# Two plain gate tiles instead of four in each SwiGLU, and q and k of the stick-breaking heads stacked by DMA

## The chip, the core and the metric

The kernel runs on one core of a Trainium2 chip. The metric is the device time of one execution in microseconds (us), the median of several runs. The engines of the core are TensorE (PE, the matmuls), VectorE (DVE), ScalarE (ACT), GpSimd (POOL) and SyncE (SP), which issues nearly all transfers. They run side by side and wait for each other by semaphores; each works through its own list of instructions in order.

## What is computed

A decoder trunk of two layers on 512 tokens of width 1024, float32. Each layer is SwiGLU, a mixer, SwiGLU; the first mixer is a hybrid of a recurrent block and attention, the second is stick-breaking attention with 16 heads of width 64.

```
def _swiglu(h, w_in, w_out):
    a, b = jnp.split(h @ w_in, 2, axis=-1)
    return (jax.nn.silu(a) * b) @ w_out
...
        z = jnp.einsum('bhqd,bhkd->bhqk', qi, k).astype(jnp.float32) * scale
        log_nb = jnp.where(mask, jax.nn.log_sigmoid(-z), 0.0)
        after = lax.cumsum(log_nb, axis=3, reverse=True) - log_nb
        w = jnp.where(mask, jnp.exp(jax.nn.log_sigmoid(z) + after), 0.0)
        return jnp.einsum('bhqk,bhkd->bhqd', w.astype(v.dtype), v)
...
    for layer in range(DEPTH):
        x = x + 0.5 * _swiglu(_rmsnorm(x, ffn_norm[layer, 0]), ffn_w_in[layer, 0], ffn_w_out[layer, 0])
        ...
        x = x + 0.5 * _swiglu(_rmsnorm(x, ffn_norm[layer, 1]), ffn_w_in[layer, 1], ffn_w_out[layer, 1])
```

The inner width of a SwiGLU is 2816, so 22 tiles of 128 (below: gate tiles, or gates 0 to 21).

## The kernel before

Activations lie transposed, features on the 128 partitions and the 512 tokens in the free dimension, in eight tiles `x`. To keep float32 accuracy with the fast matmul format every operand is split in two, a rounded high part (ScalarE's cast) and the rest (VectorE's subtraction), and each product is three matmuls (high by high, high by low, low by high). So every weight tile of 128x1024 costs a load of 512 KB, a cast and a subtraction.

**A SwiGLU** (`ffn(f, ...)`, f = 0 to 3) works on the gate tiles in two ways.

- *Plain* (`plain(j, rb)`, for j below `PLAIN`): 24 matmuls of 512 columns for the half a and 24 for the half b, on the unnormed activations `xh`, `xl`. The norm's factor of each token, `rb`, comes out during gate 0: TensorE sums squares (`rstd_parts`), GpSimd takes the root, TensorE spreads it, ScalarE copies it. `normed` multiplies the results by `rb` afterwards, and `gate` applies silu, the product of the halves, and the split of the hidden tile.
- *In pairs* (`pair(j, between, operands, before)`): two gate tiles at once (half a and half b as one block row of two) by a seven-product scheme of the Strassen kind on blocks. Each of the seven calls of `product(pt, w, o, start)` is 24 matmuls of 256 columns. Its weights are blocks a11, a12, a21, a22 or sums of them (s1 to s4: VectorE's `add`), split by `parts`. Its activations are seven operands, t0 to t6 (`ops`), blocks or sums of blocks of the normed activations, made once per SwiGLU by the generator `g_inputs(rb)`: `quarter` (four pieces of 256 columns), `less` (a difference), `put` (the split). The pair pulls one step of it ahead of each product (`next(operands, 0)`). The order of the products is: operand 0, 1, 4, 5, 2, 6 and, as `tail`, 3. The tail is run behind the first product of the next pair.

The output product (`outputs(c, done)`) of a chunk of four gates is eight tiles of 12 matmuls of 512 columns. Chunk c-1's outputs are spread between the products of the pairs of chunk c (`between(i)`, by the table `OUTPUTS`); `CHUNKS` says which gates belong to a chunk. With `PLAIN = 4` chunk 0 is plain and chunks 1 to 4 are pairs.

**Stick-breaking attention** (`stick`) goes through 8 pairs of heads. `qk_tile(p)` projects q and k of a pair (24 matmuls each); its `evac` takes the result out of the accumulator: it makes the tiles `qks` of head e and head o, each a stack of two halves of 64 partitions (for q the high part on one half and the low part on the other; for k the high part on both), and for k the low parts `klo` (named `kl0e` to `kl1o` in the trace), whose other half is zero. The score is then two matmuls, `qks` by `qks` and `qks` by `klo`. Before, the stacks are made by ScalarE copies and VectorE subtractions of 64 partitions each. `attend` runs 64 score blocks in a row; `Fill` pulls projections of later pairs and output products in between, by the due times `need`. The hybrid layer's attention makes its stacks with `stack`, four transfers issued by SyncE.

What sets the order: TensorE's order is the order of the program text (`manual_schedule`). The lists of the other engines and of SyncE are ordered by the framework's scheduler by its own estimate of times, and are fixed when the program is built. Buffers that matter here: `raw` 3 (loaded weights), `hi` and `lo` 4 each (split weights), `sum` 4, `mm` 3 and `s` 2 accumulators.

Of the kernel before, what the change touches and what calls it, by code (L numbers as in the profile page):

```python
# [10 lines left out]
F32 = mybir.dt.float32  # L11
F32R = mybir.dt.float32r
AF = mybir.ActivationFunctionType
ALU = mybir.AluOpType
AX = mybir.AxisListType

P = 128
S = 512
# [5 lines left out]
HD = 64  # L24
# [17 lines left out]

PLAIN = 4
CHUNKS = [(0, 4), (4, 8), (8, 12), (12, 16), (16, 22)]

OUTPUTS = [((0, 1, 2, 1, 1), (1, 0, 1, 0, 1)), ((0, 0, 2, 0, 2), (1, 0, 1, 0, 2)), ((0, 0, 2, 0, 2), (1, 0, 1, 0, 2)),
# [20 lines left out]
def kernel(ctx: ExitStack, tc: tile.TileContext, x, par, ffn_in, ffn_in2, ffn_out, ffn_out2,  # L69
                      hy_ug, hy_qkv, hy_qf, rg_w, hy_out, sb_qk, sb_v, sb_out, out):  # L70
    nc = tc.nc
    V, A, G, T, SY = nc.vector, nc.scalar, nc.gpsimd, nc.tensor, nc.sync
# [219 lines left out]
    def stack(st, h, l):  # L292

        top, low = slice(0, HD), slice(HD, P)
        SY.dma_start(out=st[0][top].bitcast(F32), in_=h[top].bitcast(F32))
        SY.dma_start(out=st[0][low].bitcast(F32), in_=l[top].bitcast(F32))
        SY.dma_start(out=st[1][low].bitcast(F32), in_=h[low].bitcast(F32))
        SY.dma_start(out=st[1][top].bitcast(F32), in_=l[low].bitcast(F32))
# [31 lines left out]
    def ffn(f, g_next, last=False):  # L330
# [3 lines left out]
        with ExitStack() as es:  # L334
# [233 lines left out]
            def tail():  # L568
                pass

            for c in range(1, len(CHUNKS)):
                if f == 0 and c == 3:
                    channel_consts(gp.tile([P, S], F32, tag="p5", bufs=1, name="t4"))
                g = outputs(c - 1, False)
                for j, counts in zip(range(*CHUNKS[c], 2), OUTPUTS[c - 1]):
                    def between(i):
                        for _ in range(counts[i]):
                            next(g)

                    tail = pair(j, between, operands, tail)  # L580
                if c == len(CHUNKS) - 1:
                    tail()
                run(g)
# [482 lines left out]
    def stick(g_next):  # L1066
        with ExitStack() as es:
# [9 lines left out]
            qk, vv = {}, {}  # L1077
# [5 lines left out]
            def qk_tile(p):  # L1083
                def evac(j):
                    def go(pt):
                        nonlocal rt, rb
                        if rb is None:
                            rt, rb = rstd()
                            for c, sg in enumerate((1.0, -1.0)):
                                V.tensor_scalar(out=rs[:, c], in0=rt, scalar1=sg * HD ** -0.5, scalar2=None,  # L1090
                                                op0=ALU.mult)
                        halves = [slice(0, HD), slice(HD, P)]
                        st = [mp.tile([P, S], F32R, tag=f"qk{j}{c}", bufs=2, name="qks") for c in "eo"]
                        if j == 0:

                            for t, a, b in zip(st, halves, halves[::-1]):
                                A.copy(out=t[a], in_=pt[a])
                                V.tensor_tensor(out=t[b], in0=pt[a], in1=t[a].bitcast(F32), op=ALU.subtract)
                            qk[p, j] = st
                        else:  # L1100

                            kt = wk("kt", 1)
                            V.tensor_tensor(out=kt, in0=pt, in1=rb, op=ALU.mult)
                            for t, l, a, b in zip(st, klo[p % 2], halves, halves[::-1]):
                                A.copy(out=t[a], in_=kt[a])
                                V.tensor_tensor(out=l[a], in0=kt[a], in1=t[a].bitcast(F32), op=ALU.subtract)
                                A.copy(out=t[b], in_=kt[a])
                            qk[p, j] = st
                    return go

                return [(1, 24 * US_512, g_proj(sb_qk[p, j], evac(j), on_x, KT)) for j in range(2)]
# [141 lines left out]
```

## Time and profile before

| | |
|---|---|
| median of 3 runs | 1869.08 us (1867.19 to 1870.18) |
| the profiled execution | 1865.11 us, span of its instructions 1863.4 us |
| TensorE matmul busy | 1836.0 us, 99% of the span |
| VectorE busy | 1413.3 us, 76% |
| ScalarE busy | 955.3 us, 51% |
| granted TensorE clock, mean | 1.000 |
| the chain of work that ended last | TensorE 88%, VectorE 6%, ScalarE 2% |

Times inside the trace are us from the start of the span. The four SwiGLUs lie at about 5 to 350, 575 to 930, 920 to 1270 and 1515 to 1860 us; the hybrid mixer between the first two, the stick-breaking attention from about 1270 to 1515. A timeline row gives start, duration, engine, line of the kernel, operation, output and inputs, and in brackets the idle time before it with what ended it. Instructions of one engine overlap a little in such rows, since the next starts while the last one drains; the spacing of the starts is what one costs on a busy engine.

### The profile page before, as it was taken

Reading aid. Unit: us, or ns where it says so; the run is one execution under the profiler, and the core shown is the slowest. Engines: PE = TensorE matmul, PEld = TensorE weight load, DVE = VectorE, ACT = ScalarE, POOL = GpSimd, SP = SyncE. Lnnn points to the kernel's source line nnn. Section 1 sums busy time; section 2 is a strip of 40 time slices with the busy share of each in tenths; the row PEclk is TensorE's granted clock in tenths of the full one; section 3 lists DMA queues with packets and bytes.
Section 4 is the critical chain, followed back from the end, with each engine's and each line's share of the span. In section 5 each row is a group of like instructions: output and inputs, shape, how many; then the busy total and the mean of one; then the engine's idle time right before and its main releaser. Section 6 shows DMA issues by size and latency. Waiting matters only on the chain.

```text
span 1863.4 us, 29383 instructions
## 1 busy us (share of the span) xinstructions
PE 1836.0 (99%) x11818; PEld 1664.1 (89%) x11818; DVE 1413.3 (76%) x1892; ACT 955.3 (51%) x1399; POOL 122.2 (7%) x266
## 2 busy tenths in 40 slices
PE   8999999998999999999999999999999999999999
PEld 6899999898888899999889999988888888999997
DVE  8867776688878877676597777765889978777773
ACT  5444444467755444444454444445777654444441
POOL 2000000111100000000000000001333400000000
PEclk9999999999999999999999999999999999999999
DMA  5332332353233333332323333232212123333322
GB/s 184 102 103 92 104 113 75 95 163 108 81 94 102 102 97 97 102 114 77 128 80 109 106 103 102 88 99 98 69 57 69 57 91 102 97 111 105 96 76 95
DMA packets 57304, 183.65 MB, mean 99 GB/s; under 512 B 8016, under 2 KB 9296, under 8 KB 57168
## 3 DMA queue, kind: packets, MB, share of 16 engines
q1 hardware_dynamic: 57168, 181.77, 30.6%
q8 instruction: 93, 1.52, 0.3%
q14 instruction: 43, 0.35, 0.1%
HBM read 172.31 MB, written 2.10 MB: 94 GB/s over the span
## 4 chain that ended last, share of the span: by engine, by line
PE 88%; DVE 6%; ACT 2%; issue 2%; POOL 1%; DMA 0%; SPq 0%; POOLq 0%; DVEq 0%; ACTq 0%
PE mm L457 22%; PE s L457 11%; PE mm L130 6%; PE mm L132 6%; PE mm L131 6%; PE t L457 5%; PE po L130 4%; PE po L132 4%; PE po L131 4%; PE mm L246 2%; PE mm L248 2%; PE mm L247 2%; PE mm L227 1%; PE mm L228 1%; PE mm L229 1%
## 5 line engine op out<-in xcount | busy, mean ns | idle before, releaser
L446 ACT CAST hi_w<-sum 128x1024 fp32r<-128x1024 f32 x144 | 150.8, 1050 | 191.9 <-PE s L457 52.1
L447 DVE TENSOR_TENSOR lo_w<-sum,hi_w 128x1024 fp32r<-128x1024 f32 x144 | 176.0, 1224 | 95.3 <-ACT hi_w L446 94.7
L122 ACT CAST hi_wo<-raw_wo 128x1024 fp32r<-128x1024 f32 (+1 forms) x96 | 94.1, 980 | 152.4 <-PE mm L131 64.2
L446 ACT CAST hi_w<-raw 128x1024 fp32r<-128x1024 f32 x72 | 75.8, 1052 | 129.9 <-PE s L457 70.7
L123 DVE TENSOR_TENSOR lo_wo<-raw_wo,hi_wo 128x1024 fp32r<-128x1024 f32 (+1 forms) x96 | 108.8, 1133 | 23.7 <-ACT hi_wo L122 23.7
L132 PE MATMUL po<-g,lo_wo 128*128 128x512 f32 x320 | 125.1, 391 | 1.3 <-DVE lo_wo L123 1.3
L130 PE MATMUL mm<-g,hi_wo 128*128 128x512 f32 (+1 forms) x324 | 125.8, 388 | 0.0
L130 PE MATMUL po<-g,hi_wo 128*128 128x512 f32 x320 | 125.6, 392 | 0.0
L132 PE MATMUL mm<-g,lo_wo 128*128 128x512 f32 (+1 forms) x324 | 125.5, 387 | 0.0
L131 PE MATMUL mm<-g,hi_wo 128*128 128x512 f32 (+1 forms) x324 | 125.5, 387 | 0.0
L131 PE MATMUL po<-g,hi_wo 128*128 128x512 f32 x320 | 125.2, 391 | 0.0
L122 ACT CAST hi_w<-raw_w 128x1024 fp32r<-128x1024 f32 (+2 forms) x75 | 77.9, 1040 | 85.3 <-PE mm L131 42.5
L123 DVE TENSOR_TENSOR lo_w<-raw_w,hi_w 128x1024 fp32r<-128x1024 f32 (+2 forms) x75 | 90.7, 1209 | 30.0 <-ACT hi_w L122 29.8
L549 DVE SCALAR_TENSOR_TENSOR x<-mm,x 128x512 f32<-128x512 f32 (+1 forms) x81 | 55.3, 683 | 49.8 <-PE mm L132 49.3
L246 PE MATMUL mm<-hi_w,xh 128*128 128x256 f32 (+1 forms) x312 | 90.8, 291 | 2.2 <-DVE q L897 2.2
L463 DVE TENSOR_TENSOR sum<-a,a 128x1024 f32<-128x1024 f32 x36 | 44.1, 1225 | 58.4 <-DMA a<-in_dram 58.4
L248 PE MATMUL mm<-hi_w,xl 128*128 128x256 f32 (+1 forms) x312 | 88.4, 283 | 0.0
L247 PE MATMUL mm<-lo_w,xh 128*128 128x256 f32 (+1 forms) x312 | 88.2, 283 | 0.0
L447 DVE TENSOR_TENSOR lo_w<-raw,hi_w 128x1024 fp32r<-128x1024 f32 x72 | 87.8, 1219 | 0.0
L549 DVE SCALAR_TENSOR_TENSOR x<-po,x 128x512 f32<-128x512 f32 x80 | 55.1, 689 | 39.5 <-PE po L132 39.5
L457 PE MATMUL s<-t4l,hi_w 128*128 128x256 f32 x288 | 81.6, 283 | 0.0
L457 PE MATMUL s<-t2l,hi_w 128*128 128x256 f32 x288 | 81.4, 283 | 0.0
(480 smaller groups left out, 6314.7 us busy)
## 6 DMA issues: line engine op xcount, KB each, us to landing
raw_w<-in_dram SPq DMA_DIRECT2D x72, 512.0 KB, 3.4
a<-in_dram SPq DMA_DIRECT2D x72, 512.0 KB, 3.5
raw<-in_dram SPq DMA_DIRECT2D x72, 512.0 KB, 3.5
raw_wo<-in_dram SPq DMA_DIRECT2D x64, 512.0 KB, 3.5
raw_wo<-in_dram SPq DMA_DIRECT2D x32, 384.0 KB, 3.0
raw_who<-in_dram SPq DMA_DIRECT2D x16, 512.0 KB, 3.3
qks<-hs SPq DMA_DIRECT2D x24, 128.0 KB, 2.5
x<-in_dram SPq DMA_DIRECT2D x8, 256.0 KB, 4.6
```

Of the source, the lines that this page charges most:

```text
L122: A.copy(out=hi[:, :n], in_=raw[:, :n])
L123: V.tensor_tensor(out=lo[:, :n], in0=raw[:, :n], in1=hi[:, :n].bitcast(F32), op=ALU.subtract)
L130: T.matmul(out=pt, lhsT=ah, rhs=bh, start=(start and i == 0), stop=False)
L131: T.matmul(out=pt, lhsT=ah, rhs=bl, start=False, stop=False)
L132: T.matmul(out=pt, lhsT=al, rhs=bh, start=False, stop=(stop and i == n - 1))
L246: T.matmul(out=pt, lhsT=ah, rhs=bh, start=(k == 0), stop=False)
L247: T.matmul(out=pt, lhsT=ah, rhs=bl, start=False, stop=False)
L248: T.matmul(out=pt, lhsT=al, rhs=bh, start=False, stop=(k == KT - 1))
L446: A.copy(out=hi, in_=src)
L447: V.tensor_tensor(out=lo, in0=src, in1=hi.bitcast(F32), op=ALU.subtract)
L457: T.matmul(out=po, lhsT=a, rhs=b[:, k], start=start and c + k + q == 0, stop=k == 3 and q == 2, skip_group_check=not (start and c == 0))
L549: V.scalar_tensor_tensor(out=xT[d][:, t], in0=po[:, t], scalar=0.5, in1=xT[d][:, t], op0=ALU.mult, op1=ALU.add)
```

## The change

`PLAIN` becomes 2. Gates 0 and 1 of each SwiGLU stay plain; gates 2 and 3 become a pair, run directly behind the plain tiles and without outputs in between, since chunk 0 has no chunk ahead of it. In the attention `evac` splits the whole tile of 128 partitions into `h` and `l` (named `hs` in the trace), one ScalarE copy and one VectorE subtraction, and transfers put the halves in place: four by `stack` for q; four by `stack` and two for `klo` for k.

```
-PLAIN = 4
+PLAIN = 2
...
             def tail():
                 pass
 
+            for j in range(PLAIN, CHUNKS[0][1], 2):
+                tail = pair(j, lambda i: None, operands, tail)
             for c in range(1, len(CHUNKS)):
...
-                        halves = [slice(0, HD), slice(HD, P)]
                         st = [mp.tile([P, S], F32R, tag=f"qk{j}{c}", bufs=2, name="qks") for c in "eo"]
+                        h, l = (mp.tile([P, S], F32R, tag=f"qk{c}", bufs=2, name="hs") for c in "hl")
+                        qk[p, j] = st
                         if j == 0:
 
-                            for t, a, b in zip(st, halves, halves[::-1]):
-                                A.copy(out=t[a], in_=pt[a])
-                                V.tensor_tensor(out=t[b], in0=pt[a], in1=t[a].bitcast(F32), op=ALU.subtract)
-                            qk[p, j] = st
+                            A.copy(out=h, in_=pt)
+                            V.tensor_tensor(out=l, in0=pt, in1=h.bitcast(F32), op=ALU.subtract)
+                            stack(st, h, l)
                         else:
 
                             kt = wk("kt", 1)
                             V.tensor_tensor(out=kt, in0=pt, in1=rb, op=ALU.mult)
-                            for t, l, a, b in zip(st, klo[p % 2], halves, halves[::-1]):
-                                A.copy(out=t[a], in_=kt[a])
-                                V.tensor_tensor(out=l[a], in0=kt[a], in1=t[a].bitcast(F32), op=ALU.subtract)
-                                A.copy(out=t[b], in_=kt[a])
-                            qk[p, j] = st
+                            A.copy(out=h, in_=kt)
+                            V.tensor_tensor(out=l, in0=kt, in1=h.bitcast(F32), op=ALU.subtract)
+                            stack(st, h, h)
+                            for t, a in zip(klo[p % 2], (slice(0, HD), slice(HD, P))):
+                                SY.dma_start(out=t[a].bitcast(F32), in_=l[a].bitcast(F32))
```

On TensorE, at the end of plain gate 1 of the second SwiGLU (`s` is the accumulator of its half b, `xh`, `xl` the activations, t0 operand 0). Before:

```order
L130 MATMUL s<-xh_6010,hi_w 128x512
L131 MATMUL s<-xl_6011,hi_w 128x512
L132 MATMUL s<-xh_6010,lo_w 128x512
L130 MATMUL mm<-xh_5968,hi_w 128x512
L131 MATMUL mm<-xl_5969,hi_w 128x512
L132 MATMUL mm<-xh_5968,lo_w 128x512
```

The same place after the change:

```order
L130 MATMUL s<-xh_6105,hi_w 128x512
L131 MATMUL s<-xl_6106,hi_w 128x512
L132 MATMUL s<-xh_6105,lo_w 128x512
L457 MATMUL mm<-t0h,hi_w 128x256
L457 MATMUL mm<-t0l,hi_w 128x256
L457 MATMUL mm<-t0h,lo_w 128x256
```

Where gate 2 began with the activations, the first product now begins with operand 0.

On VectorE, the list of the second SwiGLU from the split of operand 0 on (`t0l` to `t4l` are low parts of operands; `lo_w` of line 123 is a plain weight's, of line 447 a product's; `ab` and `g` are the plain tiles' norm and gate; `sum` a sum of weight blocks or of activations). Before:

```order
L408 TENSOR_TENSOR t0l<-sum,t0h 128x1024
L408 TENSOR_TENSOR t1l<-sum,t1h 128x1024
L389 TENSOR_TENSOR ab<-mm,rb 128x512
L411 TENSOR_TENSOR t3l<-t3h,sum 128x1024
L123 TENSOR_TENSOR lo_w<-raw_w,hi_w 128x1024
L351 TENSOR_TENSOR ab<-ab 128x512
L408 TENSOR_TENSOR t2l<-t6l,t2h 128x1024
L390 TENSOR_TENSOR ab<-s,rb 128x512
L463 TENSOR_TENSOR sum<-raw,a_6411 128x1024
L123 TENSOR_TENSOR lo_w<-raw_w,hi_w 128x1024
L411 TENSOR_TENSOR t3h<-t6l,t3h 128x1024
L408 TENSOR_TENSOR t4l<-t3l,t4h 128x1024
```

After:

```order
L408 TENSOR_TENSOR t0l<-sum,t0h 128x1024
L463 TENSOR_TENSOR sum<-raw,a_6364 128x1024
L408 TENSOR_TENSOR t1l<-sum,t1h 128x1024
L389 TENSOR_TENSOR ab<-mm,rb 128x512
L411 TENSOR_TENSOR t3l<-t3h,sum 128x1024
L447 TENSOR_TENSOR lo_w<-sum,hi_w 128x1024
L351 TENSOR_TENSOR ab<-ab 128x512
L408 TENSOR_TENSOR t2l<-t6l,t2h 128x1024
L390 TENSOR_TENSOR ab<-s,rb 128x512
L411 TENSOR_TENSOR t3h<-t6l,t3h 128x1024
L408 TENSOR_TENSOR t4l<-t3l,t4h 128x1024
L463 TENSOR_TENSOR sum<-sum,raw 128x1024
```

The operands keep their order and their place in the list nearly unchanged; the two plain splits are gone and a split of a product's weights stands there.

On SyncE, the transfers of the attention (`raw_w`, `raw_who` are weight loads, `qks` the stacks). Before, from the last SwiGLU output weights ahead of it to the SwiGLU behind it:

```order
L121 DMA raw_wo<-in_dram 128x768 x8
L121 DMA raw_w<-in_dram 128x1024 x24
L121 DMA raw_who<-in_dram 128x1024 x8
L121 DMA raw_w<-in_dram 128x1024 x6
L440 DMA a_16178<-in_dram 128x1024
```

After, the part that belongs to pair 6:

```order
L295 DMA qks<-hs 64x512
L297 DMA qks<-hs 64x512
L121 DMA raw_who<-in_dram 128x1024
L296 DMA qks<-hs 64x512
L298 DMA qks<-hs 64x512
L295 DMA qks<-hs 64x512
L296 DMA qks<-hs 64x512
L297 DMA qks<-hs 64x512
L298 DMA qks<-hs 64x512
L1110 DMA kl0e<-hs 64x512
L1110 DMA kl0o<-hs 64x512
L121 DMA raw_who<-in_dram 128x1024
```

Stacking transfers now stand between the weight loads, in one queue with them.

## Rows read from the trace of the kernel before

**Rows 1.** The page, part 1: busy us (share of the span) and instructions.

```profile
PE 1836.0 (99%) x11818; PEld 1664.1 (89%) x11818; DVE 1413.3 (76%) x1892; ACT 955.3 (51%) x1399; POOL 122.2 (7%) x266
```

**Rows 2.** TensorE's waits, whole run: us in total, times, longest us.

```profile
PE mm L130 <- ACT hi L321: 5.3, 1, 5.3
PE po L664 <- DVE tt L650: 4.1, 4, 1.3
...
PE po L132 <- DVE lo_wo L123: 1.3, 1, 1.3
```

**Rows 3.** Stretch: length, busy us (instructions) of PE, PEld, DVE, ACT, POOL; clock, DMA.

```profile
586.46:625.60 39.14, 39.14 (x193) 33.11 (x192) 39.14 (x52) 20.54 (x24) 0.00 (x0) 1.00 0.20 67
```

**Rows 4.** Timeline of VectorE in the second SwiGLU.

```profile
587.61 0.68 DVE L389 TENSOR_TENSOR ab<-mm,rb 128x512 f32<-128x512 f32 x1
588.21 3.25 DVE L401 SCALAR_TENSOR_TENSOR sum<-x,par_sb,rb 128x256 f32<-128x256 f32 x8
591.37 1.22 DVE L463 TENSOR_TENSOR sum<-a,a 128x1024 f32<-128x1024 f32 x1
...
597.40 1.23 DVE L408 TENSOR_TENSOR t0l<-sum,t0h 128x1024 fp32r<-128x1024 f32 x1
598.53 1.23 DVE L408 TENSOR_TENSOR t1l<-sum,t1h 128x1024 fp32r<-128x1024 f32 x1
```

**Rows 5.** Timeline of TensorE in the second SwiGLU: gate 2, first and third product.

```profile
599.48 0.39 PE L130 MATMUL mm<-xh,hi_w 128*128 128x512 f32 x1
...
621.24 0.28 PE L457 MATMUL mm<-t0h,hi_w 128*128 128x256 f32 x1
...
626.89 0.28 PE L457 MATMUL s<-t4h,hi_w 128*128 128x256 f32 x1
```

**Rows 6.** Timeline of VectorE in the first and the third SwiGLU.

```profile
26.32 1.23 DVE L123 TENSOR_TENSOR lo_w<-raw_w,hi_w 128x1024 fp32r<-128x1024 f32 x1 [1.40 <-ACT hi_w L122]
...
931.66 1.23 DVE L123 TENSOR_TENSOR lo_w<-raw_w,hi_w 128x1024 fp32r<-128x1024 f32 x1 [3.58 <-ACT hi_w L122]
```

**Rows 7.** Timeline of TensorE there: gate 2, in the first also the first product.

```profile
37.47 0.39 PE L130 MATMUL mm<-xh,hi_w 128*128 128x512 f32 x1
...
59.23 0.28 PE L457 MATMUL mm<-t0h,hi_w 128*128 128x256 f32 x1
...
944.68 0.39 PE L130 MATMUL mm<-xh,hi_w 128*128 128x512 f32 x1
```

**Rows 8.** Stretch at the run's end, columns as in rows 3.

```profile
1862.00:1863.40 1.40, 0.00 (x0) 0.00 (x0) 0.00 (x0) 0.00 (x0) 0.00 (x0) 0.56 0.00 0
```

**Rows 9.** Timeline of TensorE at the run's beginning and end.

```profile
5.85 0.63 PE L131 MATMUL mm<-xl,hi 128*128 128x512 f32 x1
6.28 0.63 PE L132 MATMUL mm<-xh,lo 128*128 128x512 f32 x1
...
1859.88 0.28 PE L132 MATMUL mm<-sum,lo_wo 128*128 128x256 f32 x1
```

**Rows 10.** Groups of lines in the attention: count | busy us, mean ns | idle before.

```profile
L1107 ACT CAST qks<-kt 64x512 fp32r<-64x512 f32 x16 | 9.9, 620 | 0.4
...
L1097 ACT CAST qks<-mm 64x512 fp32r<-64x512 f32 x16 | 9.3, 581 | 6.9 <-DVE qks L1098 6.9
```

**Rows 11.** Tile `hs` of the hybrid layer: duration ns min/median/max; transfers' landing.

```profile
L297 SPq DMA_DIRECT2D qks<-hs x8: 588/590/599, 399.9 to 521.7; - x8
...
DMA to landing us min/median/max: 2.2/2.5/4.3
```

**Rows 12.** Timeline of VectorE in the attention: `kt` of pair 6.

```profile
1437.89 0.67 DVE L1103 TENSOR_TENSOR kt<-mm,rb 128x512 f32<-128x512 f32 x1
```

**Rows 13.** Timeline of TensorE in the attention: first score of pair 6.

```profile
1442.62 0.22 PE L1129 MATMUL s<-qks 128*128 128x128 f32 x1
...
1443.92 0.52 PE L646 MATMUL t<-ident,be 128*128 128x128 f32 x3 [0.96 <-DVE be L1141]
```

**Rows 14.** SyncE's own waits in the attention, 1270 to 1530 us.

```profile
SPq L121 <- DVE lo_who L123: 69.1, 8, 10.7
```

## The prediction

> **What bounds the kernel now.** I read the page's busy shares first, then the list of who TensorE waited for, then the start of one SwiGLU in time. TensorE is busy for 1836.0 of 1863.4 us [rows 1]; its waits are few and short, and of the four SwiGLUs only the first is among them, with the program's first loads and one wait of 1.3 us later [rows 2]. So the time is TensorE's list of matmuls, and an edit can gain no more than the matmul time it takes out, unless it makes TensorE wait.
>
> The average hides the other half of the reading. At the start of the second SwiGLU, from 586.46, when the norm's factor `rb` is about there, to 625.60 VectorE has no idle time either: both engines are busy for 39.14 of 39.14 us [rows 3]. VectorE is working off a backlog there: it splits plain weights, norms and gates the plain tiles, and makes the seven operands t0 to t6 for the products. The 21.76 us of plain gates 2 and 3 are the cover under which it does so. The change takes this cover away.
>
> **The change in each SwiGLU: what TensorE saves.** Gates 2 and 3 cost TensorE the time from 599.48 to 621.24, so 21.76 us; the first product starts at 621.24 and the third at 626.89, so 2.83 us each, seven of them 19.8 us [rows 5]. The saving is 1.95 us per SwiGLU, 7.8 us in four. The bytes loaded are the same (four tiles of 512 KB either way). ScalarE gets seven more instructions net, but is busy for 20.54 us of the 39.14 [rows 3]; no cost taken.
>
> **What VectorE must do before each product.** The new order fixes VectorE's list. I add it up with the spacing of starts in the saturated stretch, where each instruction follows the last: 1.135 us for 1024 columns (597.40 to 598.53), 0.60 for 512 (587.61 to 588.21), 0.395 for each of the eight 256-column operand pieces (588.21 to 591.37); a result is there 1.23 us after the start of a wide one [rows 4]. The list begins where it began before, at 586.46, since ScalarE's cast ahead of it, which the rows name as what it waited for (the third SwiGLU's is in [rows 6]), still waits for plain gate 0.
>
> - Second SwiGLU. Ahead of t4l stand 10 wide, 5 narrow and 16 pieces: 11.35 + 3.0 + 6.32 = 20.7 us, so it starts at 607.1 and operand 4 is ready at 608.4. From there to t5l come 6 wide and 4 narrow, 9.2 us: operand 5 is ready at 617.6. After it t5l itself, one sum and t3l, 3.4 us, and the split of the fifth product's weights is ready at 621.0.
> - TensorE is free of plain gate 1 at 599.48. Products 1 and 2 find their operands (t0l starts at 597.4, t1l at 599.7) and end at 605.1. Product 3 needs operand 4: it waits 3.2 us, ends at 611.2. Product 4 needs operand 5: it waits 6.4 us, ends at 620.4. Product 5 waits 0.6. Six products end at 626.7, and the seventh, done later beside the next pair, makes it worth 629.5, against 621.24 before: **+8.2 us**. (Waits of 10.2, less the saving of 1.95.)
> - The third and fourth SwiGLU have the same list, and from its start to TensorE's free time lie the same 13.0 us (931.66 to 944.68 [rows 6, 7], the fourth alike): +8.2 each.
> - First SwiGLU: the list starts at 26.32, TensorE is free at 37.47 [rows 6, 7], 1.9 us sooner after it, and two more wide and two more narrow ones stand ahead of t4l. Operand 0 is ready at 39.2 (wait 1.8), operand 4 at 51.7 (wait 6.8), operand 5 at 59.7 (wait 5.2); seven products end at 71.0 against 59.23 [rows 7]: **+11.8**.
>
> Together +36.5 us. Afterwards VectorE has eight outputs' worth of TensorE time more per two pairs and catches up, as it does now from about 625 us on. The gates of tile 3 come later than before (its seventh product comes after the next pair's first); the first output needs them only in its last quarter, nine matmuls or 2.0 us after its start, and by the same addition they are there within 0.5 us of it: taken at 0; without that cover 1 us per SwiGLU. The 1.3 us wait of the first SwiGLU [rows 2] may go, -1.3 at best.
>
> **What the waits do to the clock.** After the first loads no wait in a SwiGLU of this trace is longer than 1.3 us [rows 2], so the price is bounded from the run's two ends. The last matmul starts at 1859.88 and the granted clock of the last 1.4 us, from 1862.0, is 0.56: it fell about 2 us after TensorE had stopped [rows 8, 9]. At the beginning matmuls of 512 columns start 0.43 us apart (1.2 GHz) [rows 9], against 0.227 in the second SwiGLU (96 in 21.76 us [rows 5]). At the lower level a product would take 2.4 us more (12 times 0.2). Bounds per long wait: 0 and 2.4. I take 1.6, two thirds of the way up, since 6.4 us of waiting is three times what was enough at the end. A slow product 3 is hidden by the wait for operand 5; a slow product 4 counts, less 0.6 that product 5 waits anyway: 3 x 1.0 + 1.6 = **+4.7** (bounds 0 and +7.8). The Trainium skill, "TensorE: Matmul & The Clock Gate", section "HAM oscillation — how this bites in real kernels", says that idle gaps between bursts of matmuls put the engine back to half rate, so that each burst starts slow: by it the sum has the clock term up to 7.8, by rows of mid-run alone it has none; no run here shows such a gap inside the kernel yet.
>
> **The change in the stick-breaking part.** Per pair ScalarE loses 2 x 0.58 for one copy and 4 x 0.62 for one, VectorE loses one narrow instruction of 0.6 us in q and one in k [rows 10]. Of TensorE's waits there, 4.1 us are four waits `po<-tt` for VectorE [rows 2], the places where such a saving can land; four times 0.6 is 2.4 us. Against it: every k tile now sends four stacking transfers and two for `klo` through SyncE, 0.59 us each to issue, 2.5 to land [rows 11]. Their place is tightest in pair 6: `kt` is made by 1438.56, its copy by 1439.2, the fifth transfer issues at 1441.6 and lands at 1444.1, where the score begins at 1442.62 now [rows 12, 13]: 1.4 us late, of which 0.96 is a wait that stands right behind it anyway [rows 13]. I count 0.9 for it; every other pair has at least 1.4 us more room. The weight loads on SyncE stand ahead of these transfers, and SyncE waits up to 10.7 us for a free buffer there [rows 14]; two stacks caught behind that would cost some 8 us. So -4.1 to +8, and I take -2.4 + 0.9 = **-1.5**.
>
> **Sum.** 36.5 + 4.7 - 1.5 = +39.7 us on the profiled execution of 1865.1, so 1904.8. The median of the runs shown, 1869.1, lies 4.0 higher; the forecast for the median is **1909**.
>
> **Rivals.**
> 1. *The clock stays low.* If after each wait TensorE's level recovers only once a whole pair has run, products 4 to 6 and the next one take 2.4 us more each; some 3 to 4 us a SwiGLU over my term: 1921. For it: two long waits within 18 us. Against: from 621 us on nothing makes TensorE wait.
> 2. *SyncE's queue holds the stacked q and k back.* +8 in place of -1.5: 1918. For it: 69.1 us of waiting for `lo_who` on that queue [rows 14]. Against: the hybrid layer stacks q and k the same way today, and no score there is among TensorE's waits [rows 2].
> 3. *Faster: VectorE's backlog doesn't reach TensorE.* If operands 4 and 5 came in time, the four SwiGLUs would give 7.8 us and the attention 1.5: 1860. It decides from the point at which the waits of one SwiGLU fall below 1.95 us, so VectorE's 31 us of list up to t5l would have to take 23 or less. For it: TensorE has never waited there so far. Against: VectorE's list is fixed, in order and without a gap already.
> 4. *The q and k edit does not shorten anything*, since its waits are for other things: 1910, no case of its own.
>
> **How the numbers follow.** Forecast 0.77, rival 1 0.11, rival 2 0.06, rival 3 0.05; 0.01 for a tie. Lower end: no clock term, -4.1 in the attention, -1.3 in the first SwiGLU, 1869.1 + 31.1 = 1900, and 3 for errors of the addition: 1897. Upper end: 1869.1 + 36.5 + 7.8 + 8 = 1921.4: 1922. Rival 3 and the slower part of rival 1 stay outside, about 1 in 10. A measurement here tells 0.2%, 3.7 us, from no change: faster 0.05, same 0.02, slower 0.93.
>
> **What would show it.** TensorE's list of waits should show products (line 457 of before) waiting for `t4l`, `t5l` of VectorE, some 10 us a SwiGLU in two pieces of 3 and 6 us, and busy time in those stretches falling under 75%. VectorE should be without idle time from `rb` to the pair's last split. The SwiGLU from `rb` to the first output should be 8 us longer. The clock may fall in four or eight places. In the attention, `po<-tt` waits should shrink, and at most pair 6 wait for a transfer. It is wrong if products 3 and 4 start without a wait, if VectorE idles while TensorE waits (then a load or ScalarE is the cause), or if scores wait for `qks` in more than two pairs.

## The result, and the profile after

The changed kernel takes 1908.88 us (median of 4 runs, 1908.17 to 1909.38), the kernel before on the same chip 1868.13 us (1867.10 to 1870.18): a ratio of 1.0222, 95% interval 1.021 to 1.0235. It is slower by 40.75 us; forecast were 1909 and slower. The profiled execution took 1909.23 us, its span is 1907.5 us, 44.1 more than the span before (1863.4).

TensorE's share of the span fell from 99% [rows 1] to 97%, and its list of waits has new heads. First the busy times of the page, then the waits of the whole run (engine and line, what was waited for: us in total, times, longest us):

```profile
PE 1846.1 (97%) x12106; PEld 1685.4 (88%) x12106; DVE 1433.8 (75%) x1900; ACT 956.0 (50%) x1395; POOL 119.3 (6%) x266
```

```profile
PE mm L457 <- DVE t5l L408: 14.8, 4, 4.3
PE s L457 <- DVE t4l L408: 13.9, 4, 4.9
...
PE mm L457 <- DVE ab L488: 3.3, 2, 2.2
PE mm L457 <- ACT t5h L407: 3.1, 2, 1.6
...
PE s L1132 <- DMA kl0e<-hs: 1.9, 1, 1.9
...
PE po L131 <- DVE g L360: 1.3, 3, 0.4
```

In rows 2 no product stood among the waits. Now operands 4 and 5 do, four times each, once in every SwiGLU, and two that the prediction's sum doesn't have: the seventh product waits for `ab` (line 488, the sum that frees its accumulator), the first output for `g`, the gate of tile 3. The start of the second SwiGLU as TensorE's timeline shows it (start, duration; in brackets the wait and what ended it):

```profile
612.14 0.28 PE L457 MATMUL mm<-t0h,hi_w 128*128 128x256 f32 x1
...
621.08 0.39 PE L457 MATMUL s<-t4l,hi_w 128*128 128x256 f32 x1 [3.01 <-DVE t4l L408]
625.63 0.39 PE L457 MATMUL mm<-t5h,hi_w 128*128 128x256 f32 x1 [1.55 <-ACT t5h L407]
630.30 0.58 PE L457 MATMUL mm<-t5l,hi_w 128*128 128x256 f32 x1 [4.28 <-DVE t5l L408]
634.49 0.28 PE L457 MATMUL s<-t2h,hi_w 128*128 128x256 f32 x1
645.33 0.39 PE L457 MATMUL mm<-t3h,hi_w 128*128 128x256 f32 x1 [2.18 <-DVE ab L488]
657.06 0.50 PE L131 MATMUL po<-g,hi_wo 128*128 128x512 f32 x1 [0.42 <-DVE g L360]
```

VectorE's timeline in the same SwiGLU, the first row being the start of its list. It has no gap up to 637; the first, at 637.59, is 0.47 us, and the first long one is at 640.58, where a sum of the second pair's weights waits for a load. That load was issued at 636.02, when VectorE had split (until 635.99) what lay in its only buffer, and took 4.5 us to land. `ab`, for which the seventh product waits, stands behind that sum in the queue:

```profile
599.12 1.23 DVE L447 TENSOR_TENSOR lo_w<-raw,hi_w 128x1024 fp32r<-128x1024 f32 x1 [3.58 <-ACT hi_w L446]
...
619.81 1.22 DVE L408 TENSOR_TENSOR t4l<-t3l,t4h 128x1024 fp32r<-128x1024 f32 x1
...
637.59 0.69 DVE L488 TENSOR_TENSOR ab<-s,keep 128x512 f32<-128x512 f32 x1 [0.47 <-PE s L457]
640.58 1.22 DVE L463 TENSOR_TENSOR sum<-a,a 128x1024 f32<-128x1024 f32 x1 [2.29 <-DMA a<-in_dram]
...
644.59 0.68 DVE L488 TENSOR_TENSOR ab<-mm,keep 128x512 f32<-128x512 f32 x1
```

The stretches from the first product to the end of the first output, in the second and the third SwiGLU, and 2 us inside the wait for `t5l` (columns as in rows 3):

```profile
612.14:657.63 45.49, 34.05 (x253) 32.15 (x252) 40.90 (x43) 22.45 (x28) 0.00 (x0) 0.92 0.28 94
969.77:1013.36 43.59, 36.31 (x254) 34.51 (x253) 40.90 (x43) 22.55 (x28) 0.00 (x0) 0.88 0.30 98
```

```profile
628.00:630.00 2.00, 0.00 (x0) 0.00 (x0) 2.00 (x2) 0.81 (x1) 0.00 (x0) 0.50 0.00 0
```

VectorE has 40.90 us of work in each, of 45.49 and 43.59 us. TensorE's work is shorter: 34 to 36 us, part of it at the lower clock, 0.50 (1.2 GHz) while it waits. In the rest of the 45.49 us VectorE mostly waits, 2.29 us for that load and 1.17 for a cast. In these stretches VectorE's list, with what it waits for, is the bound, in the rest of the run TensorE, and the shares of 97% and 75% show neither.

From one SwiGLU's mark (the matmul that spreads the norm's factor) to the next, the spans grew by 11.8, 12.4, 10.5 and 11.3 us for the four SwiGLUs, by 1.4 in the hybrid layer, which has no edit, and shrank by 2.7 in the stick-breaking layer and by 0.5 at the start: 44.1 together.

### The profile page after: what moved, and what is told of

Its sections match the earlier page's. It is cut to its first block, busy times and chain, and to the rows that moved or that the text cites. A ratio compares the mean times of both kernels' runs of the same rounds, so it can differ in the third digit from the quotient of the medians.

```text
span 1907.5 us, 30140 instructions
## 1 busy us (share of the span) xinstructions
PE 1846.1 (97%) x12106; PEld 1685.4 (88%) x12106; DVE 1433.8 (75%) x1900; ACT 956.0 (50%) x1395; POOL 119.3 (6%) x266
## 4 chain that ended last, share of the span: by engine, by line
PE 83%; DVE 11%; issue 3%; ACT 1%; DMA 1%; POOL 1%; SPq 0%; POOLq 0%; DVEq 0%; ACTq 0%
PE mm L457 22%; PE s L457 11%; PE t L457 5%; PE mm L131 5%; PE mm L130 5%; PE mm L132 5%; PE po L131 4%; PE po L132 4%; PE po L130 4%; PE mm L246 2%; PE mm L248 2%; PE mm L247 2%; DVE lo_w L447 1%; PE mm L227 1%; PE mm L228 1%
## 5 line engine op out<-in xcount | busy, mean ns | idle before, releaser
L446 ACT CAST hi_w<-sum 128x1024 fp32r<-128x1024 f32 x160 | 167.2, 1050 | 223.1 <-DVE sum L463 65.8
L447 DVE TENSOR_TENSOR lo_w<-sum,hi_w 128x1024 fp32r<-128x1024 f32 x160 | 195.0, 1223 | 106.8 <-ACT hi_w L446 106.1
L457 PE MATMUL mm<-t5l,hi_w 128*128 128x256 f32 x320 | 93.0, 291 | 14.8 <-DVE t5l L408 14.8
L457 PE MATMUL s<-t4l,hi_w 128*128 128x256 f32 x320 | 93.3, 292 | 13.9 <-DVE t4l L408 13.9
L457 PE MATMUL mm<-t5h,hi_w 128*128 128x256 f32 x320 | 92.8, 290 | 3.1 <-ACT t5h L407 3.1
L457 PE MATMUL s<-t4h,hi_w 128*128 128x256 f32 x320 | 92.1, 288 | 1.3 <-ACT t4h L407 1.3
L457 PE MATMUL mm<-t3h,hi_w 128*128 128x256 f32 x320 | 89.6, 280 | 3.4 <-DVE ab L488 3.3
L457 PE MATMUL mm<-t5h,lo_w 128*128 128x256 f32 x320 | 92.3, 289 | 0.0
L457 PE MATMUL mm<-t0l,hi_w 128*128 128x256 f32 x320 | 90.0, 281 | 1.5 <-DVE t0l L408 1.5
L457 PE MATMUL s<-t4h,lo_w 128*128 128x256 f32 x320 | 91.4, 286 | 0.0
```

Of the source, the lines that this page charges most:

```text
L446: A.copy(out=hi, in_=src)
L447: V.tensor_tensor(out=lo, in0=src, in1=hi.bitcast(F32), op=ALU.subtract)
L457: T.matmul(out=po, lhsT=a, rhs=b[:, k], start=start and c + k + q == 0, stop=k == 3 and q == 2, skip_group_check=not (start and c == 0))
```

## The experiments

Theory: VectorE's ordered list sets when the products can start, and what was its cover is gone. Rivals: loads or ScalarE's casts hold the products; the fall of the clock is the loss; SyncE's queue holds q and k back.

**Runs 1 and 2: each half of the change alone.**

```diff
 run 1: PLAIN = 2, with the old q and k
 run 2: the new q and k, with
-PLAIN = 2
+PLAIN = 4
```

> The changed kernel with the old q and k: only the SwiGLU part of the change is left. By my theory that part holds all of the loss and a little more: in the traces of before and after the four SwiGLUs grew by 11.8, 12.4, 10.5 and 11.3 us and the attention shrank by 2.7, so this run should take about 2.7 us more than the changed kernel, 1911, that is 43 us over the kernel before. Rival, the q and k edit costs something through SyncE's queue: then this run is faster than the changed kernel, 1900 to 1907. TensorE's four waits po <- tt, 4.1 us in all before and 0.6 us after, should be back.

> The kernel before with only the new q and k: four gates stay plain products. By my theory it gains 2.7 us, 1865.4 against 1868.1 (ratio 0.9986), with the waits po <- tt shrunk from 4.1 to about 0.6 us and a new wait of about 2.4 us of one score for the low halves of k in pair 6. Rival of the prediction, the stacks stuck behind weight loads on SyncE: 8 us slower, 1876. Rival, the edit shortens nothing: 1868, ratio 1.000.

Run 1: 1910.99 us, ratio 1.024 (1.0226 to 1.0254). Run 2: 1862.48 us against 1866.02, ratio 0.9983 (0.9974 to 0.9992), so about 3 us faster. The waits of run 1, then those of run 2:

```profile
PE po L666 <- DVE tt L652: 4.1, 4, 1.3
```

```profile
PE s L1132 <- DMA kl0e<-hs: 1.5, 1, 1.5
...
PE po L666 <- DVE tt L652: 0.5, 2, 0.4
```

The halves add up. The SwiGLU part holds the whole loss. In run 2's attention the `po<-tt` waits of rows 2 fell from 4.1 to 0.5 us and those for `be` from 1.7 to 0.6, against 1.9 of two scores that wait for low halves of `k`: 2.8 of the 3.3 us by which its span shrank. SyncE's queue holds nothing back for long: that rival is out.

**Run 3: VectorE's list shorter.** The four differences of the input are left out.

```diff
-                less(t, b12, b11)
-                put(4, t)
+                put(4, b12)
 ... (operands 5, 6 and 3 alike)
```

> The changed kernel without the four differences of the normed input (operands 3 to 6 are cast and split from plain blocks; this part of the computation is left out): VectorE's list up to the fifth product is 4 wide instructions or 4.5 us shorter, nothing else of it moves. By my theory (VectorE's list is what the products wait for) the waits for t4l go, those for t5l or the weights after it shrink to about 4.4 us, and each SwiGLU is about 4.5 us shorter, with less loss of clock as well: 1909 less 18 to 24, so 1885 to 1891. Rival, the loads or ScalarE's casts hold the products: these are the same here, so 1909. Rival, the loss is the clock alone: the waits are still there, and the gain is at most the 1 to 2 us a SwiGLU of the clock, 1901 to 1905.

1900.97 us (1899.30 to 1906.21), 7.9 less than the changed kernel: the direction is right, the size less than half. The waits of the profiled execution, with 1906.21 us the slowest of the four:

```profile
PE mm L453 <- DVE lo_w L443: 9.0, 4, 2.3
PE mm L453 <- ACT hi_w L442: 7.0, 4, 2.1
...
PE po L131 <- DVE g L360: 4.1, 4, 1.0
PE po L130 <- ACT g L359: 4.0, 4, 1.0
```

The waits for `t5l` are gone and of those for `t4l` 0.2 us are left, as expected. The time is the one that the rival of the clock named (1901 to 1905), but that rival keeps these waits. Product 4 now waits for its weights (the cast and split of a sum), and the first output for both parts of the gate, 2.0 us in each SwiGLU. The second SwiGLU reached product 5 after 17.2 us instead of 22.4, but the end of the first output came only 3.6 us sooner after its first product. Work taken off one place of the list comes back as a wait for a later place.

**Runs 4 and 5: two more wide VectorE instructions, in the changed kernel and in the one before.**

```diff
-                less(t, b12, b11)
+                for _ in range(3):
+                    less(t, b12, b11)
```

> The changed kernel with two more 1024-wide VectorE instructions in each SwiGLU, ahead of operand 4 (the first difference is made three times). 2 x 1.135 = 2.3 us more on VectorE's list per SwiGLU; besides, the scheduler puts the split of some weights ahead of t5l here. By my theory every us on that list is a us of the whole: at least 2.3 and up to 5 us per SwiGLU, 1918 to 1929. Rival, VectorE is not the bound (loads or ScalarE): 1909, as the changed kernel, since VectorE is busy for only 75% of the span.

> The same two more 1024-wide VectorE instructions per SwiGLU, now in the kernel before, where four gates are plain products. By my theory the matmuls of gates 2 and 3 cover VectorE's list: operand 4 is ready near 611 and is needed at 626.9, so 4.5 us more VectorE work in each SwiGLU costs nothing: 1867, ratio 0.999 to 1.002. In the changed kernel the same instructions cost 20 us. Rival, VectorE's work costs time wherever it stands: 10 to 20 us here too, 1876 to 1888.

Run 4: 1929.02 us, 20.1 more than the changed kernel, 5.0 per SwiGLU. Run 5: 1866.65 us, ratio 1.000 (0.9991 to 1.0009) to the kernel before. The same work costs 20 us without the plain gates and nothing behind them. In run 5, second SwiGLU, VectorE's row is `t4l`, TensorE's the first use of operand 4:

```profile
617.99 1.22 DVE L408 TENSOR_TENSOR t4l<-t3l,t4h 128x1024 fp32r<-128x1024 f32 x1
...
629.04 0.28 PE L458 MATMUL s<-t4h,hi_w 128*128 128x256 f32 x1
```

Operand 4 is there at 619.2, some 10 us before its product. This pair settles that the cover was what the change took away. It doesn't price a microsecond of the list by itself: in run 4 the scheduler also moved other instructions ahead of `t4l`, whose start lies 27.6 us behind the list's instead of 20.7, for 2.3 us of added work.

**Run 6: the clock.** Matmuls that nobody reads fill TensorE's waits.

```diff
+            def busy(j, n):
+                if j == PLAIN:
+                    po = psum("po", 1)
+                    for i in range(n):
+                        T.matmul(out=po, lhsT=xh[i % KT][:, :P], rhs=xh[i % KT], start=True, stop=True)
 ...
+                busy(j, 11)
                 product(pz, w5, 4, True)
 ...
+                busy(j, 20)
                 product(px, w6, 5, False)
```

> The changed kernel with added matmuls that nobody reads, ahead of products 3 and 4 of the first pair in each SwiGLU: 11 and 20 of 512 columns, some 2.5 and 4.5 us at full clock, 28 us in four SwiGLUs. TensorE then works while it waited. By my theory the waits are free time and their cost beyond themselves is the clock: the added 28 us cost nothing, the clock stays near 1.00 in the SwiGLUs, and each SwiGLU is 0.8 to 2 us shorter than in the changed kernel: 1901 to 1906. Rival, the fall of the clock costs nothing since product 4 waits anyway: 1909. Rival, the waits are not idle time of TensorE that work can fill: up to 28 us more, 1937.

1910.66 us (1907.72 to 1911.52): no gain in the whole. The third SwiGLU, the same stretch as above (43.59 us at a clock of 0.88 in the changed kernel):

```profile
968.39:1011.81 43.42, 39.75 (x284) 36.41 (x283) 40.86 (x43) 22.45 (x28) 0.00 (x0) 1.00 0.28 98
```

The clock is 1.00, TensorE works 3.4 us more, and the stretch is as long as before: 43.42 us around 40.86 us of VectorE. Product 5 began 1.5 us sooner after the first product than in the changed kernel (20.98 for 22.50), but the seventh product began 31.1 us after it, for 31.3: it waited 0.95 us for `ab`, which stands behind a load in VectorE's queue. In the fourth the gain lasted to the first output, which waited 2.0 us for the gate, and the stretch is as long as before. The second is 2.5 us shorter, but 1.4 of it because the load landed in 3.1 instead of 4.5 us, and 1.1 because in VectorE's list a split stands ahead of the sum that waits for the load, where it stood behind. The first is 1.3 longer: the fill outlasted its second wait by 0.3, the first output waited the rest, and the clock there was still 0.93. The four together are 1.4 us shorter.

The whole time doesn't show even that. In this execution the attention, which the edit doesn't touch, took 3.8 us longer than in the changed kernel's: the score of pair 6 waited 3.1 instead of 1.9 us, and the clock was 0.54 in the 7 us from there:

```profile
PE s L1140 <- DMA kl0e<-hs: 3.1, 1, 3.1
```

```profile
1477.00:1484.00 7.00, 6.67 (x24) 5.91 (x25) 2.16 (x6) 2.66 (x7) 1.71 (x6) 0.54 0.20 72
```

So by the SwiGLUs alone my theory of the clock (0.8 to 2 us from each) holds for what comes up to product 5, and not for the end. I suspected the waits behind it (the seventh product, the gate) of taking the gain back, and tried once more with those relieved.

**Runs 9 to 11: the waits behind.**

```diff
 run 9
-                a21, a22 = load(src[1, 0], gp, "a21", 1), load(src[1, 1], gp, "a22", 1)
+                a21, a22 = load(src[1, 0], gp, "a21", 2), load(src[1, 1], gp, "a22", 2)
 run 10, besides
-OUTPUTS = [((0, 1, 2, 1, 1), (1, 0, 1, 0, 1)), ...
+OUTPUTS = [((0, 0, 2, 1, 2), (1, 0, 1, 0, 1)), ...
 run 11, besides
+                busy(j, 20 if f == 0 else 11)
                 product(pz, w5, 4, True)
 ...
+                busy(j, 9 if f == 0 else 18)
                 product(px, w6, 5, False)
```

> The changed kernel with two buffers instead of one for the two lower blocks of a pair's weights, so that the second pair's are loaded before the first pair has split its own. In the changed kernel VectorE stood idle for 2.29 us in the second SwiGLU until that load was there, with the sum that frees the seventh product's accumulator behind it in its queue, and the seventh product waited 2.18 and 1.14 us in two SwiGLUs. By my theory (load, in order ahead of that sum) those waits go, 3.3 us and a little of what stands behind them: 1904 to 1906. Rival, the seventh product is late because VectorE's backlog isn't worked off: the waits move to the gate g of the first output and the time stays at 1909.

> Run 9's kernel, and the first output of each SwiGLU one place later in the second pair (behind the fourth product instead of the third there), so that the gate of tile 3 has 2.8 us more. In the changed kernel the first output took 3.84 us instead of 2.9 in each SwiGLU, some of it a wait for that gate. By my theory (the gate was not hidden, 0.9 us a SwiGLU) it gains 3.6 us on run 9: 1900 to 1903. Rival, VectorE's backlog reaches further and the wait moves along: no gain on run 9.

> Run 10's kernel with the unread matmuls of run 6 (11 and 18 of 512 columns ahead of products 3 and 4, 20 and 9 in the first SwiGLU), which keep the clock up. Run 6 showed a clock of 1.00 and no gain. If that was because waits behind the seventh product and the first output took the time back, those are relieved here, and the clock's part shows: 1.6 to 2.5 us in each SwiGLU less than run 10, 1893 to 1896. Rival, the low clock in products 3 and 4 costs nothing since what product 5 waits for sets the end: the same as run 10.

Run 9: 1917.65 us, 8.8 *slower* than the changed kernel; neither theory had that. From mark to mark the first and the third SwiGLU are 3.0 and 5.3 us longer than in the changed kernel, the fourth 0.3, and the second is 0.2 shorter. In the second the wait of the seventh product is gone, but with the load there sooner the scheduler put the second pair's sum ahead of `t4l`, and TensorE's wait for `t4l` grew from 3.01 to 4.14 us, by just that instruction's 1.13 us. VectorE's two rows, then TensorE's:

```profile
622.87 1.21 DVE L463 TENSOR_TENSOR sum<-a,a 128x1024 f32<-128x1024 f32 x1
624.00 1.21 DVE L408 TENSOR_TENSOR t4l<-t3l,t4h 128x1024 fp32r<-128x1024 f32 x1
...
625.27 0.58 PE L457 MATMUL s<-t4l,hi_w 128*128 128x256 f32 x1 [4.14 <-DVE t4l L408]
```

In the first the split of plain gate 1's weights went behind operand pieces (VectorE starts it at 34.42 instead of 25.74) and TensorE waited for it; in the third the first output waited for the gate, which stood behind a sum that waited for a load. The two waits:

```profile
35.69 0.57 PE L132 MATMUL s<-xh,lo_w 128*128 128x512 f32 x1 [3.51 <-DVE lo_w L123]
...
1019.57 0.79 PE L131 MATMUL po<-g,hi_wo 128*128 128x512 f32 x1 [2.61 <-DVE g L360]
```

This isn't the clean test of the load that it was meant to be. Run 10: 1909.27 us, 8.4 less than run 9, 5.1 of it in the third SwiGLU, 0.9 and 1.2 in the second and the fourth and nothing in the first, where 0.9 was expected in each; on the changed kernel alone the later output wasn't tried. Run 11: 1908.61 us, ratio 1.0232 (1.0217 to 1.0247) beside run 10's 1.0234 (1.0217 to 1.0251) on the same chip. The third SwiGLU from the first product to the first output's end, run 10, then run 11:

```profile
971.56:1018.11 46.55, 37.91 (x277) 36.80 (x276) 43.63 (x46) 24.32 (x30) 0.00 (x0) 0.89 0.27 91
```

```profile
971.15:1017.43 46.28, 41.70 (x307) 38.84 (x305) 43.09 (x45) 23.90 (x30) 0.00 (x0) 1.00 0.26 91
```

In run 11 product 6 began 1.3 us sooner after the first product than in run 10, and the first output gave most of it back: it waited 0.72 us for a split of its weights by VectorE. In the second SwiGLU 2.0 us became 0.9 in the same way; in the first and the fourth the clock was still 0.93 and 0.96. All four together are 0.9 us shorter, where 1.6 to 2.5 in each was expected. So a second time most of what the full clock gave was lost behind. The rows again have VectorE at 43 of 46 us.

**Runs 7 and 12: GpSimd beside VectorE.** GpSimd is nearly idle; run 7 gives it the differences and the first pair's sums.

```diff
 def less
-                    V.tensor_tensor(out=out, in0=a, in1=b, op=ALU.subtract)
+                    G.tensor_tensor(out=out, in0=a, in1=b, op=ALU.subtract)
 def pair, where j == PLAIN: s1 to s4 likewise
```

> The changed kernel with eight wide instructions of each SwiGLU moved from VectorE to GpSimd: the four differences of the input and the four sums of the first pair's weights. GpSimd is busy for 6% of the span; I estimate 3.2 us for one of 1024 columns from its rows of 512 columns, 1.6 us. By my theory, VectorE being what the products wait for, operand 4 comes in time, operand 5 about 1.6 us late, and the fifth product's weights wait for GpSimd's last sum, ready near 615.7: each SwiGLU is about 5 us shorter than in the changed kernel, 1886 to 1892 (run 3 took out 4.5 us of VectorE per SwiGLU and gained 8 us, so 1895 if the rest shows up late at the output as there). Rival, the two engines slow each other: VectorE's spacing of 1.135 us would grow while GpSimd runs, and the gain is lost: 1909 or more.

1932.02 us: 23 slower than the changed kernel, where 17 to 23 faster was expected. VectorE's rows in the second SwiGLU, then GpSimd's (POOL) there:

```profile
616.85 0.68 DVE L390 TENSOR_TENSOR ab<-s,rb 128x512 f32<-128x512 f32 x1
617.45 2.04 DVE L401 SCALAR_TENSOR_TENSOR t6l<-x,par_sb,rb 128x256 f32<-128x256 f32 x1
...
622.08 3.41 DVE L408 TENSOR_TENSOR t1l<-sum,t1h 128x1024 fp32r<-128x1024 f32 x1
```

```profile
616.21 2.99 POOL L411 TENSOR_TENSOR t3l<-t3h,sum 128x1024 f32<-128x1024 f32 x1 [6.51 <-DVE t3h L401]
621.16 3.24 POOL L411 TENSOR_TENSOR t3h<-t6l,t3h 128x1024 f32<-128x1024 f32 x1 [1.96 <-DVE t6l L401]
```

GpSimd's second instruction ends at 624.40, and `t1l`, issued at 622.08, at 625.49: 1.09 us later, about its spacing of 1.135 when alone. So it did nothing while GpSimd ran. The piece at 617.45 took 2.04 instead of 0.4 us, until shortly after GpSimd's end at 619.20. The instruction at 616.85, with one input in PSUM, took its 0.68 beside the same GpSimd instruction. The Trainium skill, "GPSIMD Engine Reference", section 8 "Key points", says that the two engines share their SBUF interfaces and contend where a VectorE instruction has two SBUF inputs; these rows agree. But the chain of run 7 is longer too (GpSimd's last sum comes late), so run 12 separates the two: GpSimd works beside the list and nobody needs the result.

```diff
+                aside = gp.tile([P, KT // 2, 256], F32, tag="aside", bufs=1, name="aside")
+                h = ops[0][0].bitcast(F32)
+                for _ in range(3):
+                    G.tensor_tensor(out=aside, in0=h, in1=h, op=ALU.subtract)
```

> The changed kernel with three more GpSimd instructions of 1024 columns in each SwiGLU, whose result nobody reads, started when operand 0 is cast, in the stretch in which VectorE has no idle time. Nothing is taken from VectorE. In run 7 VectorE's instructions with two inputs in SBUF were stretched from 1.2 to 3.3 us while GpSimd worked. If GpSimd holds VectorE back, the three, some 2.4 to 3.3 us each, cost 6 to 9 us of VectorE's time per SwiGLU and TensorE waits for t4l that much longer: 1933 to 1945. Rival, run 7 was slow because GpSimd's sums are slow and stood in the chain: no change here, 1909.

1924.70 us, 15.8 more than the changed kernel, 4.0 per SwiGLU, less than the 6 to 9 expected: no longer chain, and yet slower. VectorE's row, GpSimd's, and TensorE's first wait in the second SwiGLU:

```profile
609.48 5.98 DVE L401 SCALAR_TENSOR_TENSOR t3h<-x,par_sb,rb 128x256 f32<-128x256 f32 x4
```

```profile
607.63 7.16 POOL L418 TENSOR_TENSOR aside<-t0h 128x1024 f32<-128x1024 f32 x3 [6.68 <-ACT t0h L407]
```

```profile
619.97 0.39 PE L461 MATMUL mm<-t0l,hi_w 128*128 128x256 f32 x1 [3.24 <-DVE t0l L408]
```

Four pieces of operand 3 took 5.98 us instead of 1.6. The 7.16 us of GpSimd cost VectorE 4.3: `t0l` starts 15.27 us behind the list's start, 10.95 in the changed kernel. The SwiGLUs grew by 4.5, 3.2, 4.3 and 4.5. This is also the cleanest price of the list, with no reordering: 4.3 us of VectorE, 4.0 us of the whole.

**Run 8: q and k alone, the transfers of `k` head by head.**

```diff
-                            stack(st, h, h)
-                            for t, a in zip(klo[p % 2], (slice(0, HD), slice(HD, P))):
-                                SY.dma_start(out=t[a].bitcast(F32), in_=l[a].bitcast(F32))
+                            hs = slice(0, HD), slice(HD, P)
+                            for t, lo, a, b in zip(st, klo[p % 2], hs, hs[::-1]):
+                                SY.dma_start(out=t[a].bitcast(F32), in_=h[a].bitcast(F32))
+                                SY.dma_start(out=t[b].bitcast(F32), in_=h[a].bitcast(F32))
+                                SY.dma_start(out=lo[a].bitcast(F32), in_=l[a].bitcast(F32))
```

> The kernel before with the new q and k only (as run 2), the six transfers of a k tile put head by head: both halves and the low half of head 0 first, then those of head 1. In run 2 one score waited 1.5 us for the low half of k of head 0, which is fifth in the queue; here it is third and goes 2 x 0.59 us sooner. By my theory that wait shrinks to about 0.3 us: 1.2 us less than run 2, 1861.3, ratio 0.9975 to the kernel before. Rival, the wait merely moves to the next thing that pair needs (be of VectorE stood behind it with 1 us before): the same as run 2, 1862.5.

1861.63 us against 1866.00, ratio 0.998 (0.997 to 0.9989): faster than both kernels, with four plain gates as before. Against run 2's 0.9983 the difference is within the intervals. The trace shows that the wait for the low half of `k` became one for `be`, which stood behind it:

```profile
PE s L1134 <- DVE be L1145: 1.0, 1, 1.0
```

## Why the prediction was right, point by point

**The cover.** Right, by runs 4, 5, 9 and 12. The reading that carried it was rows 3: both engines busy for 39.14 of 39.14 us, so neither had room for what the other lost.

**The waits of the SwiGLU.** Forecast for the second: 3.2 for operand 4, 6.4 for operand 5, 0.6 for product 5. Measured: 3.01, 1.55 + 4.28 = 5.83, and none. Product 3's first wait ended 8.94 us after the first product's start, forecast 8.9; product 4's 18.16, forecast 18.1. Adding up a saturated engine's list by spacings of rows 4 was good to 0.1 us. In the first SwiGLU the waits were 1.5, 6.2 and 2.6, forecast 1.8, 6.8 and 5.2; operand 5 was used 22.24 us after TensorE was free of the plain gates, forecast 22.2, and the third wait is shorter mostly because product 3, at the low clock, filled it.

**The clock.** It fell in every SwiGLU, as foreseen, to 0.50 in the waits or right behind them, and slowed products 3 and 4: beyond their waits and 2.99 us each they took 2.0 us more in the second SwiGLU and 4.5 in the third. The Trainium skill's section "HAM oscillation — how this bites in real kernels" of "TensorE: Matmul & The Clock Gate" is borne out in that, which before no row could show. Up to product 5 the term of +4.7 (its working, 3 x 1.0 + 1.6, gives 4.6) was right: by the forecast list alone product 5 starts 21.5 us after TensorE is free of the plain gates, 25.1 in the first SwiGLU, and it started 1.5, 0.8, 1.0 and 0.7 us later in the four, 4.1 together. But it isn't what the clock costs. The step that failed is "a slow product 4 counts". It took product 5's split as the last thing that VectorE delays; VectorE's list goes on to the first output, 40.9 of the 43 to 45 us, with a load in it that waits for VectorE, and most of what a product gains by ending sooner is lost in waits there. With the clock back in the second to fourth SwiGLU (run 6) product 5 began 1.3 to 1.5 us sooner, and at the first output's end 0.2 us of that were left in the third and nothing in the fourth; the second gained by its load and its order. In run 11 0.9 and 0.3 us were left in the second and the third. In the first neither run kept the clock up, so its part there stays open.

**The gates taken at 0, and what comes later.** This is the same error from the other side. The prediction gave the gates of tile 3 no cost, since VectorE "catches up", and named 1 us per SwiGLU without that cover. The first output took 3.84 to 3.86 us instead of 2.9 in the last three SwiGLUs, so 0.9 each; in the first it took 2.9. The seventh product's waits, 2.18 and 1.14 us in the second and fourth, are not in the prediction at all: a load whose single buffer comes free late held VectorE's queue, with `ab` behind it. With these two, 2.7 and 3.3 us, the growth of the four SwiGLUs adds up: 36.5 of the list and 4.1 up to product 5, less the 1.3 us wait of the first SwiGLU, which is gone as the prediction allowed, are 45.3 of the 46.0 measured; forecast were 41.2 (36.5 + 4.7). Run 9 shows that the load's wait can be moved, not what it costs by itself; this stays open.

**q and k.** Forecast -1.5, measured -2.7 in the spans and about -3 in run 2's ratio. Of the 4.1 us of waits 3.5 went, where 2.4 was taken, and of those for `be` 1.1; the score of pair 6 waited 1.9, where 0.9 was taken, and one of pair 7, which should have had room, 0.5.

**The sum.** From profile to profile the spans grew by 44.1 us, forecast 39.7; the medians by 40.75. The hit on the median is partly luck: the profiled execution before lay 3 us under its median, the one after lay at its own, and the 4.0 us that the forecast added for the step from the profiled execution to the median made up for the 4.4 missed.

**The rivals.** The clock didn't stay low: from 634 to 636 us it was back at 1.00. SyncE's queue held one score for 1.9 us and one for 0.5, not 8. VectorE's backlog reached TensorE in all four SwiGLUs. And q and k did shorten something.

## What to carry to other kernels

Where two engines are both full in a stretch, work taken off the one that bounds the run is no gain until the other's list, added up row by row, fits the shorter cover; the shares of the whole run (99% and 76%) say nothing on that. In such a stretch most of what the engine that waits gains, by its clock too, is lost at its next wait (here at most 0.9 us of it were left in a SwiGLU), and the list must be followed to where that engine really has caught up, here past the last operand to the first output. A buffer that lets a load start sooner can let a scheduler put its consumer ahead of something more urgent.

## What the runs showed of the hardware

GpSimd holds VectorE back: 7.16 us of GpSimd cost VectorE 4.3 us, instructions with two inputs in SBUF stood still (1.2 became 3.4 us), one with an input in PSUM did not (0.68 us). Not every one with two inputs did: `sum<-a,a` of run 12, begun at 607.74, 0.11 us behind GpSimd's first, took its usual 1.22 us. And GpSimd was held back too: in run 7 an instruction of 1024 columns took 2.40 us while VectorE was idle, and 2.67 to 3.32 beside it in the same SwiGLU. An idle GpSimd was no free help to a full VectorE.

The same gap doesn't always lower the clock. In the hybrid layer TensorE waits 1.1 and 1.6 us close behind each other, before and after alike. The 4 us behind it, of the kernel before, then of the one after:

```profile
430.11:434.11 4.00, 4.00 (x21) 3.40 (x22) 2.28 (x5) 3.97 (x8) 0.31 (x1) 1.00 0.24 95
```

```profile
441.40:445.40 4.00, 4.00 (x13) 3.27 (x14) 2.05 (x4) 3.97 (x8) 0.31 (x1) 0.60 0.21 82
```

With equal work ahead the clock stayed at 1.00 once and fell to 0.60 once; in run 2, with the SwiGLUs of before, it fell too (0.63). This is part of the 1.4 us by which the hybrid layer grew without an edit, and a likely part of the 3 us by which the profiled execution before lay under its median. Why one execution escapes it stays open.
